# Hybrid decoder layer on one Trainium2 core: the convolution's pointwise weights and its half of the output weights multiplied once on the chip, the second token tile's output projection in one piece, operand transposes issued later

## The chip, the cores and the metric

The kernel runs on one core of a Trainium2 chip. The metric is device time in microseconds (us): the median of three runs before the change is 2017.57 us (2012.16, 2017.57 and 2020.62).

## The reference

One decoder layer over 2048 tokens of width 1024, in float32:

```
hn   = rms_norm(x, mix_pre_g);  proj = hn @ w_in        # 1024 x 1792
attn = sliding-window attention of q, k, v              # 512 columns
u    = the other 1024 columns of proj
conv = silu(layer_norm(depthwise_conv31(a * sigmoid(gate)))) @ w_conv_pw   # 512 x 512
h    = x + rms_norm(concat(attn, conv) @ w_out, mix_post_g)
ff   = (silu(rms_norm(h) @ w_gate) * (rms_norm(h) @ w_up)) @ w_down
out  = h + rms_norm(ff, ffn_post_g)
```

Between the pointwise product with `w_conv_pw` and the product with rows 512 to 1023 of `w_out` there is no other operation.

## The kernel before, in words

**Tiles and precision.** The tokens are four tiles (t = 0 to 3) of 512. Each float32 operand of a large product is held as a high part and a low part (`split_w`, L129: ScalarE copies the high part, GpSimd or VectorE subtracts to get the low part), and a product is three matmuls: high by high, high by low, low by high (`three`, L188). One matmul is 128x128 weights by 128x512. A low part of a weight may be written to memory the first time and read back later (`lo_in`, `lo_out`).

**Stages.** The letter after the @ in a tile's name is the stage, the digit its token tile.
- A0 to A3 (`stage_a`, L327): input projections, 14 units of 24 matmuls each.
- B0 to B3 (`stage_b`, L430): attention in four blocks of 128 tokens. Each block goes through score matmuls, VectorE, exponentials on ScalarE, transposes on TensorE and a mask on GpSimd; its result goes to `mixT[0:4]` in memory.
- C0 to C3: the convolution. `stage_taps` (L563) does 31 taps for each of four channel groups on VectorE and writes to `y_scr`. `stage_tail` and `conv_tail` (L577, L592) load it, transpose on TensorE into the one PSUM bank `ct`, take the statistics, normalise, transpose back, apply swish (`v`, L616), split `v`, and then do the pointwise product: for each of four output groups m, load `w_pw[m]`, split it, 12 matmuls into `ct`, copy out with scale 0.5, write to `mixT[4+m]` from ScalarE's queue (L623 to L631).
- W0 to W3 (`stage_w`, L697): output projection. It walks the eight 128-row blocks of `mixT` and of `w_out` in four pairs `gi` and two column halves n, 24 matmuls each, adding into `acc`; `norm_w` (L747) then norms, adds x and writes `hn_scr`.
- H, F, G (for token tiles 0 and 1, then again, as H2, F2, G2, for 2 and 3): the feed-forward layer, its products arranged in sums of blocks. `stage_h_plain` (L829) makes operands B11 and B21 from `hn_scr` with transposes, `stage_h_sums` (L842, "S0") the others. `stage_pre` (L887) and `stage_p1` are F, `stage_p2` is G.

**What sets the order.** A main line of stages is passed to `run`, and at each of its yields, which carry a nominal time, side lanes (`Lane`, L1275) are pumped: `lb` attention, `lc` taps, `ld` tails C0 and C1, `lw` W0 and later C2, W2, C3, W3, `lh` the H stages and W1's norm (N1), which is offered when W1's last matmul is issued; S0 also waits until F0 has reached its unit 22. A lane works through its items in order and only when an item's condition holds. The order that results is a priority; a scheduler then places the instructions on each engine, and each engine runs its own in that order. The main line is A0 to A3, then W1, then F0 (`stage_pre`, `stage_p1`), G0 and the second half. C0 and W0 run beside A2 and A3, C1 beside A3 and W1, C2, W2, C3 and W3 beside G0.

**W1's stop.** In W1, after the attention half of the rows (`G * gi + G == 4`), the main line runs the first eight units of F0 (`ready`, Q0 = 8, L734 to L740), 12 matmuls each, and in their middle calls `ld.until("C1")`, which issues what is left of C1. Only then does W1 take the convolution half. The rest of F0 follows W1. Because these eight units need operand B11, B11 and B21 are offered to lane `lh` before W1 with no condition (L1417).

Of the kernel before, what the change touches and what calls it, by code (L numbers as in the profile page):

```python
# [23 lines left out]
D = 1024  # L24
DFF = 2816
P = 128
# [11 lines left out]
def layer_kernel(ctx, tc, x, xT, cols, rows, sinks, relb, onehot, w_in, w_pw, w_out, w_gate, w_up, w_down, out):  # L38
# [190 lines left out]

    mixT = dr.tile([KC, P, S], F32, name="mixT")  # L230
    h_scr = dr.tile([S, D], F32, name="h_scr")

    neg = cst.tile([P, 1], F32, name="neg")
    nc.vector.memset(neg, NEG)
# [357 lines left out]
    def conv_tail(t, yt):  # L592
        L = f"C{t}"
        lab[0] = L
        mv = sm(8).rearrange("p (s a) -> p s a", a=2)
        for s in range(4):
            st = sm(6)
            nc.vector.bn_stats(st, yt[:, s])
            nc.vector.bn_aggr(mv[:, s], st)
        r = rsqrt(mv[:, :, 1], 4, 1.0)  # L600
        nmr = sm(4)
        stt(nmr, mv[:, :, 0], -1.0, r, ALU.mult, ALU.mult)
        yield YL if t < 2 else YL2
# [3 lines left out]
        sc = []  # L607
        for c in range(4):
            b = ct()
            for s in range(4):  # L610
                nc.tensor.transpose(b[:, s * P : (s + 1) * P], yt[:, s, c * P : (c + 1) * P], ident)
            th = f2("fc")
            act(th, b, AF.Tanh, scale=lnh[:, c : c + 1], bias=lnh[:, 4 + c : 5 + c])
            v = f2("fc")
            act(v, b, AF.Identity, scale=ln_g[:, c : c + 1], bias=ln_b[:, c : c + 1])
            stt(v, th, 1.0, v, ALU.add, ALU.mult)  # L616
            h = hl("chl")
            act(h[:, 0], v, AF.Copy)
            ptt(h[:, 1], v, h[:, 0].bitcast(F32), ALU.subtract)
            sc.append(h)  # L620
            yield 2
            lab[0] = L
        for m in range(4):  # L623
            raw = f2("fc")
            nc.sync.dma_start(raw, w_pw[m])
            w = split_w(raw, "mb" if t == 1 and m % 2 else "chl").rearrange("p a (k c) -> p a k c", c=P)
            o = ct()
            three(o, [((w[:, 0, k], w[:, 1, k]), (sc[k][:, 0], sc[k][:, 1])) for k in range(4)])
            z = f2("gb" if t > 1 else "fc")
            act(z, o, AF.Copy, scale=0.5)  # L630
            nc.scalar.dma_start(mixT[4 + m, :, t * T : (t + 1) * T], z)  # L631
            yield 2
            lab[0] = L

    bias = []

# [60 lines left out]
    def stage_w(w, spill, G, atag, htag, mtag, bank_of, norm=None, ready=None):  # L697
        L = f"W{w}"
        lab[0] = L
        acc = [f4(atag) for _ in range(4)]  # L700
# [22 lines left out]
        for gi in range(KC // G):  # L723
            aa = nxt
            for n in range(2):
                lab[0] = L
                if n == 0 and w != 1 and gi + 1 < KC // G:
                    rows_next = load(gi + 1)
                if n == 1 and gi + 1 < KC // G and not (ready and G * gi + G == 4):
                    nxt = acts(gi + 1, rows_next if w != 1 else None)  # L730
                ws = weight(w_out[2 * gi : 2 * gi + 2, :, n * T : (n + 1) * T].rearrange("c p t -> p c t"),
                            lo_out[n, 2 * gi : 2 * gi + 2], w > 0)
                yield from block_half(acc, list(zip(aa, ws)), n, gi == 0, L, bank_of)
            if ready and G * gi + G == 4:  # L734
                for i, c in enumerate(ready()):
                    if i == Q0 // 2:
                        ld.until("C1")
                        lab[0] = L
                        nxt = acts(gi + 1)
                    yield c  # L740
        tail = norm_w(w, spill, acc, mtag)
        if norm:
            norm(tail)
# [590 lines left out]
    NS = 12  # L1334
    AHEAD = 3
    PRES = {0: 20, 2: 16}
    Q0 = 8
    POOL_LO = (3, 6)
    PRE_S0, PRE_S2 = 22, 16
    H1, H2, H3, H4 = 0, 4, 7, 11  # L1340
    lb = Lane(RB, 0)
    lc = Lane(RC0, LC)
    lw = Lane(RW0, 0)
# [161 lines left out]
```

## Time and profile before

| what | value |
|---|---|
| median of three runs | 2017.57 us |
| profiled execution, span | 2016.4 us, the only time of it that the profile gives |
| matmuls and transposes in the profiled span | 8826 |
| 128x512 matmuls of the pointwise product (`ct@C`) | 192, 48 for each token tile |
| mean granted TensorE clock | 0.991 of full |
| memory traffic | 223 GB/s over the span |

The span runs from the first to the last instruction. PE is TensorE, PEld its weight loads, DVE is VectorE, ACT is ScalarE, POOL is GpSimd, SP is the engine that issues most transfers. A timeline row gives start, duration, engine, line, operation, tiles out<-in with shape and count, and in brackets the idle time before it with what ended it. A row of windows gives each engine's busy time in a stretch, with the number of instructions, the granted clock and the share of the transfer engines.

### The profile page before, as it was taken

The page shows a single profiled execution, that of the slowest core. Times are in us where ns is not written, and L with a number is a line of the kernel's source. Part 1 is how long each engine was busy: PE and PEld are TensorE (multiplying, and loading weights), DVE is VectorE, ACT ScalarE, POOL GpSimd, SP SyncE. Part 2 cuts the span into 40 slices and gives each one's busy share as a digit, 9 for nine tenths or more (in the row PEclk, how much of TensorE's full clock was granted, in tenths as well). Part 3 has the DMA queues.
Part 4 walks back from the last instruction along what each step waited for, and adds up shares of the span by engine and source line. Part 5 has one row for each costly group of instructions (what it writes and reads, how often), then busy time and mean ns, then how long its engine had stood idle before and what let it go on. Part 6 is the DMA issues. An engine that isn't in the chain of part 4 may idle for free. (4 is left out here: it accounts for less than half of the span.)

```text
span 2016.4 us, 27154 instructions
## 1 busy us (share of the span) xinstructions
PE 1957.8 (97%) x8826; PEld 1563.3 (78%) x8826; DVE 1489.5 (74%) x2679; ACT 985.7 (49%) x1938; POOL 355.0 (18%) x415
## 2 busy tenths in 40 slices
PE   8999999999998999999989999999899999999998
PEld 7877767677667778888878878778688888888886
DVE  5998987985794899888569984475766765545558
ACT  5455455457546633333355466456643343345543
POOL 6000223322110300000001022103523332221000
PEclk9999999999999999999989999999999999999999
DMA  8786645669559878777476778579944443366654
GB/s 309 267 298 221 207 148 175 194 228 322 180 178 325 281 238 269 253 253 254 149 239 216 238 261 283 173 262 348 333 159 167 157 160 107 107 238 214 200 187 162
DMA packets 234110, 451.44 MB, mean 224 GB/s; under 512 B 23496, under 2 KB 49264, under 8 KB 233968
## 3 DMA queue, kind: packets, MB, share of 16 engines
q1 hardware_dynamic: 211184, 411.96, 60.9%
q10 hardware_dynamic: 20544, 30.42, 4.1%
q0 software_dynamic: 2240, 7.34, 0.9%
q8 instruction: 69, 1.13, 0.2%
q14 instruction: 73, 0.60, 0.1%
HBM read 330.60 MB, written 119.02 MB: 223 GB/s over the span
## 5 line engine op out<-in xcount | busy, mean ns | idle before, releaser
L85 DVE SCALAR_TENSOR_TENSOR fc@C<-glu@C,colt,fc@C 128x512 f32<-128x512 f32 x480 | 367.8, 780 | 3.0
L108 PE MATMUL mm@F<-hl@H,w@F 128*128 128x512 f32 x1056 | 254.9, 392 | 5.3 <-ACT mm@F L924 4.9
L108 PEld LDWEIGHTS mm@F<-hl@H,w@F 128*128 128x128 f32 x1056 | 198.5, 189 | 48.8 <-ACT mm@F L924 6.7
L108 PE MATMUL mm@G<-hl@G,hl@G 128*128 128x512 f32 x924 | 228.0, 396 | 6.4 <-DVE x@G L85 4.3
L108 PE MATMUL mm@A<-hl@A,w@A 128*128 128x512 f32 x840 | 206.3, 396 | 3.0 <-ACT hl@A L318 1.2
L108 PEld LDWEIGHTS mm@G<-hl@G,hl@G 128*128 128x128 f32 x924 | 174.1, 190 | 44.5 <-issue 4.1
L797 ACT ACTIVATE w@F<-chl@F 128x512 fp32r<-128x512 f32 x220 | 135.6, 625 | 135.3 <-PE mm@F L108 123.3
L108 PE MATMUL mm@G<-w@G,hl@G 128*128 128x512 f32 x876 | 199.5, 389 | 0.0
L108 PEld LDWEIGHTS mm@G<-w@G,hl@G 128*128 128x128 f32 x876 | 164.4, 188 | 34.1
L108 PEld LDWEIGHTS mm@A<-hl@A,w@A 128*128 128x128 f32 x840 | 154.7, 188 | 39.4 <-DVE hl@A L85 3.0
L85 DVE TENSOR_TENSOR w@F<-chl@F,w@F 128x512 fp32r<-128x512 f32 x198 | 144.9, 733 | 34.7 <-ACT w@F L797 34.3
L108 PE MATMUL mm@F<-mid@H,w@F 128*128 128x512 f32 x528 | 131.1, 393 | 7.4 <-ACT mm@F L924 7.2
L108 PE MATMUL mm@F<-p@H,w@F 128*128 128x512 f32 x528 | 129.1, 389 | 0.8 <-ACT at@F L1046 0.8
L108 PE MATMUL mm@F<-ql@H,w@F 128*128 128x512 f32 x528 | 127.2, 389 | 0.7 <-ACT w@F L797 0.7
L108 PE MATMUL mm@F<-x@H,w@F 128*128 128x512 f32 x528 | 125.5, 391 | 0.0
L108 PEld LDWEIGHTS mm@F<-mid@H,w@F 128*128 128x128 f32 x528 | 98.3, 188 | 30.2 <-ACT mm@F L924 9.0
L108 PEld LDWEIGHTS mm@F<-p@H,w@F 128*128 128x128 f32 x528 | 98.9, 188 | 21.9 <-ACT at@F L1046 1.4
L108 PEld LDWEIGHTS mm@F<-ql@H,w@F 128*128 128x128 f32 x528 | 99.0, 188 | 21.6 <-ACT w@F L797 1.1
L108 PEld LDWEIGHTS mm@F<-x@H,w@F 128*128 128x128 f32 x528 | 98.7, 188 | 21.0
L108 PE MATMUL tr@W<-w@W,ql@W 128*128 128x512 f32 x384 | 103.0, 408 | 8.4 <-ACT ql@W L706 5.1
L133 ACT ACTIVATE w@A<-raw@A 128x512 fp32r<-128x512 f32 x110 | 67.7, 626 | 78.8 <-PE mm@A L108 51.5
L108 PE MATMUL mm@W<-w@W,hl@W 128*128 128x512 f32 x384 | 101.5, 404 | 2.2 <-ACT x@W L679 0.7
(302 smaller groups left out, 3337.0 us busy)
## 6 DMA issues: line engine op xcount, KB each, us to landing
mids<-fa@F SPq DMA_DIRECT2D x154, 256.0 KB, 2.7
raw@A<-w_in SPq DMA_DIRECT2D x55, 512.0 KB, 4.4
w@A<-lo_in SPq DMA_DIRECT2D x84, 256.0 KB, 3.5
fc@G<-mids SPq DMA_DIRECT2D x77, 256.0 KB, 3.5
fa@G<-mids SPq DMA_DIRECT2D x75, 256.0 KB, 4.5
gb@F<-keeps SPq DMA_DIRECT2D x72, 256.0 KB, 4.3
raw@W<-w_out SPq DMA_DIRECT2D x32, 512.0 KB, 5.5
w@W<-lo_out SPq DMA_DIRECT2D x48, 256.0 KB, 4.4
```

The source lines that it names most:

```text
L85: r = op(*args, **kw)
L108: r = nc.tensor.matmul(*args, **kw)
L133: act(w[:, 0], raw, AF.Copy)
L797: act(w[:, 0], x, AF.Copy)
```

## The change

W = 0.5 x `w_conv_pw` @ `w_out[512:1024]` is computed once on the chip, in a new stage J0 of 96 matmuls, and written in eight 128x512 pieces to `w_join` in memory. W0 to W3 read `w_join` where they read rows 512 to 1023 of `w_out`, and the convolution tails write `v` itself to `mixT`; the pointwise product goes. J0 stands in lane `ld` ahead of C0 and starts once A2 has. W1 has no stop, F0 starts at its first unit after W1, and B11 and B21 wait until W0 has been done for a nominal 24 us. On the host `w_conv_pw` is laid out transposed.

```diff
@@ conv_tail
             stt(v, th, 1.0, v, ALU.add, ALU.mult)
-            h = hl("chl")
-            act(h[:, 0], v, AF.Copy)
-            ptt(h[:, 1], v, h[:, 0].bitcast(F32), ALU.subtract)
-            sc.append(h)
+            nc.sync.dma_start(mixT[4 + c, :, t * T : (t + 1) * T], v)
             yield 2
-        for m in range(4):
-            raw = f2("fc")
-            nc.sync.dma_start(raw, w_pw[m])
-            w = split_w(raw, "mb" if t == 1 and m % 2 else "chl").rearrange("p a (k c) -> p a k c", c=P)
-            o = ct()
-            three(o, [((w[:, 0, k], w[:, 1, k]), (sc[k][:, 0], sc[k][:, 1])) for k in range(4)])
-            z = f2("gb" if t > 1 else "fc")
-            act(z, o, AF.Copy, scale=0.5)
-            nc.scalar.dma_start(mixT[4 + m, :, t * T : (t + 1) * T], z)
-            yield 2
+    def stage_join():
+        right = []
+        for k in range(4):
+            raw = f4("wx", (P, 2, T))
+            nc.sync.dma_start(raw, w_out[4 + k].rearrange("p (a b) -> p a b", a=2))
+            yield 1.5
+            for n in range(2):
+                right.append(split_w(raw[:, n], "mid" if k < 2 else "chl"))
+            yield 1.5
+        for mp in range(2):
+            pair_ = t_("yt", (P, 2, 2, T), F32R)
+            raw = f4("wx", (P, 2, T))
+            nc.sync.dma_start(raw, w_pw[2 * mp : 2 * mp + 2].rearrange("m p t -> p m t"))
+            yield 1.5
+            left = [split_w(raw[:, m], pair_[:, m]).rearrange("p a (k c) -> p a k c", c=P) for m in range(2)]
+            yield 2
+            for m in range(2):
+                for n in range(2):
+                    o = ct()
+                    three(o, [((left[m][:, 0, k], left[m][:, 1, k]), (right[2 * k + n][:, 0], right[2 * k + n][:, 1])) for k in range(4)])
+                    z = f2("fa")
+                    act(z, o, AF.Copy, scale=0.5)
+                    nc.scalar.dma_start(w_join[2 * mp + m, :, n * T : (n + 1) * T], z)
+                    yield 4
@@ stage_w
-                if n == 1 and gi + 1 < KC // G and not (ready and G * gi + G == 4):
+                if n == 1 and gi + 1 < KC // G:
+                    if w == 1 and G * gi + G == 4:
+                        ld.until("C1")
                     nxt = acts(gi + 1, rows_next if w != 1 else None)
-                ws = weight(w_out[2 * gi : 2 * gi + 2, :, n * T : (n + 1) * T].rearrange("c p t -> p c t"),
+                src = w_out[2 * gi : 2 * gi + 2] if gi < 2 else w_join[2 * gi - 4 : 2 * gi - 2]
+                ws = weight(src[:, :, n * T : (n + 1) * T].rearrange("c p t -> p c t"),
-            if ready and G * gi + G == 4:
-                for i, c in enumerate(ready()):
-                    if i == Q0 // 2:
-                        ld.until("C1")
-                        nxt = acts(gi + 1)
-                    yield c
@@ the main line
+    ld.add("J", stage_join(), lambda: "A2" in started)
-        lh.add(n + ".0", stage_h_plain(ws, ops, n, off))
-    run(stage_w(1, True, 2, "mid", "hl", "at", mm, norm=lambda g: lh.add("N1", g), ready=lambda: stage_pre(ws, ops, mids[0], keeps[0], 0, Q0)))
+        lh.add(n + ".0", stage_h_plain(ws, ops, n, off), lambda: since(lw, "W0", NH))
+    run(stage_w(1, True, 2, "mid", "hl", "at", mm, norm=lambda g: lh.add("N1", g)))
-    lh.until("B21.0")
-    run(stage_pre(ws, ops, mids[0], keeps[0], Q0))
+    run(stage_pre(ws, ops, mids[0], keeps[0]))
@@ kernel
-    wp = kblocks(f(w_conv_pw))
+    wp = kblocks(f(w_conv_pw).T)
```

More of the change, by code (lines that the diff above doesn't have):

```diff
@@ L231, in layer_kernel @@
     h_scr = dr.tile([S, D], F32, name="h_scr")
+    w_join = dr.tile([4, P, D], F32, name="w_join")
     neg = cst.tile([P, 1], F32, name="neg")
@@ L606, in conv_tail @@
             act(yt[:, s], yt[:, s], AF.Identity, scale=r[:, s : s + 1], bias=nmr[:, s : s + 1])
-        sc = []
         for c in range(4):
@@ L616, in conv_tail @@
             stt(v, th, 1.0, v, ALU.add, ALU.mult)
-            h = hl("chl")
-            act(h[:, 0], v, AF.Copy)
-            ptt(h[:, 1], v, h[:, 0].bitcast(F32), ALU.subtract)
-            sc.append(h)
+            nc.sync.dma_start(mixT[4 + c, :, t * T : (t + 1) * T], v)
             yield 2
             lab[0] = L
-        for m in range(4):
-            raw = f2("fc")
-            nc.sync.dma_start(raw, w_pw[m])
-            w = split_w(raw, "mb" if t == 1 and m % 2 else "chl").rearrange("p a (k c) -> p a k c", c=P)
-            o = ct()
-            three(o, [((w[:, 0, k], w[:, 1, k]), (sc[k][:, 0], sc[k][:, 1])) for k in range(4)])
-            z = f2("gb" if t > 1 else "fc")
-            act(z, o, AF.Copy, scale=0.5)
-            nc.scalar.dma_start(mixT[4 + m, :, t * T : (t + 1) * T], z)
-            yield 2
-            lab[0] = L
+    def stage_join():
+        lab[0] = "J0"
+        right = []
[4 more added lines that the diff above has]
+            for n in range(2):
+                lab[0] = "J0"
+                right.append(split_w(raw[:, n], "mid" if k < 2 else "chl"))
+            yield 1.5
+            lab[0] = "J0"
+        for mp in range(2):
[3 more added lines that the diff above has]
+            yield 1.5
+            lab[0] = "J0"
+            left = [split_w(raw[:, m], pair_[:, m]).rearrange("p a (k c) -> p a k c", c=P) for m in range(2)]
+            yield 2
+            for m in range(2):
+                for n in range(2):
+                    lab[0] = "J0"
+                    o = ct()
[4 more added lines that the diff above has]
+                    yield 4
+                    lab[0] = "J0"
     bias = []
@@ L695, in post_scale, with stage_w @@
             tied(stt(acc[:, cs], acc[:, cs], r, gb[n], ALU.mult, ALU.mult))
-    def stage_w(w, spill, G, atag, htag, mtag, bank_of, norm=None, ready=None):
+    def stage_w(w, spill, G, atag, htag, mtag, bank_of, norm=None):
         L = f"W{w}"
@@ L1336, in layer_kernel @@
     PRES = {0: 20, 2: 16}
-    Q0 = 8
     POOL_LO = (3, 6)
@@ L1340, in layer_kernel @@
     H1, H2, H3, H4 = 0, 4, 7, 11
+    NH = 24
     lb = Lane(RB, 0)
```

2 lines of the change are left out of this document (1 added, 1 removed).

## The prediction

> **What bounds the kernel now.** I read the page first: engine totals, the slices, the chain that ended last.
>
> ```profile
> span 2016.4 us, 27154 instructions
> PE 1957.8 (97%) x8826; PEld 1563.3 (78%) x8826; DVE 1489.5 (74%) x2679; ACT 985.7 (49%) x1938; POOL 355.0 (18%) x415
> PE   8999999999998999999989999999899999999998
> DVE  5998987985794899888569984475766765545558
> PEclk9999999999999999999989999999999999999999
> ```
>
> TensorE is busy 97% of the span and in nearly every slice; no other engine is above 74%. So a matmul more or less costs its own time, and what remains to be won elsewhere is the 58.6 us (2016.4 less 1957.8) in which TensorE sits idle, plus what a lowered clock loses. The next view is the windows of 100 us; columns are the stretch, its length, then busy time and count for each engine, granted clock, transfer share, GB/s.
>
> ```profile
> 200.00:300.00 100.00, 97.12 (x483) 71.48 (x482) 89.38 (x200) 49.58 (x120) 21.20 (x24) 0.98 0.57 184
> 300.00:400.00 100.00, 98.91 (x469) 70.89 (x467) 88.27 (x190) 50.33 (x136) 34.68 (x36) 1.00 0.55 177
> 500.00:600.00 100.00, 92.13 (x435) 67.66 (x436) 85.00 (x179) 51.51 (x126) 10.24 (x12) 0.98 0.55 184
> 1100.00:1200.00 100.00, 97.54 (x432) 79.18 (x431) 95.09 (x154) 46.56 (x85) 9.29 (x17) 1.00 0.75 250
> 1500.00:1600.00 100.00, 100.00 (x443) 82.81 (x442) 65.75 (x85) 39.44 (x70) 31.40 (x21) 1.00 0.47 166
> ```
>
> The row at 1500 has no idle time: 443 matmuls in 100 us, 0.2257 us each. That is my price of a 128x512 matmul that is taken out of or put into a full stretch. The row at 500 (W1 with its stop, C1, B3, the first operand transposes) is the least full of the five. In the row at 1100, beside C2 and the last taps, VectorE is at 95%.
>
> **The change, part by part.** The pointwise matmuls, from the view of their tile, and the splits they need:
>
> ```profile
> L108 PE MATMUL ct@C<-chl@C,chl@C x168: 388/389/795, 288.1 to 1274.0; 128*128 128x512 f32 x168
> L108 PE MATMUL ct@C<-chl@C,mb@C x24: 387/392/502, 499.2 to 525.3; 128*128 128x512 f32 x24
> L135 POOL TENSOR_TENSOR chl@C<-fc@C,chl@C 128x512 fp32r<-128x512 f32 x14 | 19.5, 1396 | 73.6 <-ACT chl@C L133 73.6
> fc@C<-w_pw SPq DMA_DIRECT2D x16, 256.0 KB, 4.6
> ```
>
> 1. *Removed:* 168 + 24 = 192 matmuls, 48 for each token tile. *Added:* J0 has 8 groups of 12, 96. C0's and C1's 96 go from the stretch between 288 and 526 us, and J0's 96 come into A2, in the same stretch or a little ahead of it, where TensorE is 97% to 99% busy: an exchange, 0. C2's and C3's 96 go from G0 without replacement: 96 x 0.2257 = **-21.7 us**. ScalarE, GpSimd and the transfers lose work (28 activations and 20 GpSimd splits fewer, 16 loads of 256 KB replaced by six of 512 KB); they are not the bound, so nothing for that. VectorE's work stays the same.
>
> 2. *What the stops cost now.* TensorE's timeline, in the places that the change touches, and one row after each gap:
>
> ```profile
> 506.96 0.66 PE L815 MATMUL tr@H<-ident,fa@H 128*128 128x128 f32 x4 [2.52 <-ACT gb@H L835]
> 509.46 3.56 PE L108 MATMUL ct@C<-chl@C,chl@C 128*128 128x512 f32 x10 [0.30 <-POOL chl@C L135]
> 523.13 2.54 PE L108 MATMUL ct@C<-chl@C,mb@C 128*128 128x512 f32 x10
> 577.91 0.66 PE L500 MATMUL tr@B<-ident,p@B 128*128 128x128 f32 x4 [3.36 <-DVE p@B L85]
> 581.42 3.01 PE L108 MATMUL mm@W<-w@W,hl@W 128*128 128x512 f32 x12 [0.58 <-DVE hl@W L85]
> 637.31 7.36 PE L108 MATMUL mm@F<-hl@H,w@F 128*128 128x512 f32 x24 [2.75 <-ACT mm@F L924]
> ...
> 1027.69 7.25 PE L108 MATMUL tr@W<-w@W,ql@W 128*128 128x512 f32 x18 [3.27 <-ACT mid@W L679]
> ...
> 1289.51 0.94 PE L108 MATMUL tr@W<-w@W,ql@W 128*128 128x512 f32 x2 [2.15 <-ACT ql@W L706]
> 1290.24 1.49 PE L108 MATMUL mm@G<-hl@G,hl@G 128*128 128x512 f32 x3
> 1291.53 3.98 PE L108 MATMUL tr@W<-w@W,ql@W 128*128 128x512 f32 x13
> 1295.34 3.34 PE L108 MATMUL mm@G<-hl@G,hl@G 128*128 128x512 f32 x14
> ```
>
> A gap costs more than itself, since the clock is lower after it. The ten matmuls at 509.46 took 3.56 us where ten at 523.13 took 2.54: the gap of 2.52 cost 3.5. The 24 at 637.31 took 7.36 against 24 x 0.2257 = 5.4: the gap of 2.75 cost 4.7. The 18 at 1027.69 took 7.25 against 4.1: the gap of 3.27 cost 6.4. From 1289.51 to 1295.34, 18 matmuls took 5.8 against 4.1: the gap of 2.15 cost 3.9. After 3.36 us at 577.91 there is no such loss.
>
> [...]
>
>    - *Operand transposes later, C1's pointwise product gone.* The gap of 2.52 waited for ScalarE's copy of an H0 transpose, queued beside exponentials and C1's copies. In the changed order the same 32 transposes stand in groups of four between runs of W1's matmuls, and W0's `hn_scr` is old by then. I count the gap, its slow clock and some 1.4 us of smaller gaps beside it: **-5**.
>    - *N1 has eight units more.* W1's norm now starts at F0's unit 0 instead of unit 8, so it is out of ScalarE's queue when the second half of the units begins (unit 20), which is where the 2.75 us stood. S0 still begins at unit 22. Between 0 and 4.7 I take half: **-2.3**.
>    - *One hop fewer ahead of W3.* The gap of 2.15 is the end of this chain:
>
> ```profile
> 1278.00 1.00 ACT mm@G L1210 x2
> 1279.00 0.53 ACT gb@C L630
> 1279.55 5.01 DMA mixT<-gb@C
> 1284.62 4.18 DMA at@W<-mixT
> ```
>
>    The write and the read of `mixT` stay (`v` now takes them), but four load-split-multiply-copy rounds through the one bank `ct` go: **-3.9**. Late next is the read of `mixT`, up to 4 us, with G0's own matmuls beside it.
>
> 3. *W1 without its stop.* The eight F0 units, 8 x 12 x 0.2257 = 21.7 us of work that waited for nothing of B3, stood between W1's halves. They are not lost, only later, and B3 now reaches about seven units into F0, so they still cover its last block. But W1's 192 matmuls run beside three blocks of B3 and taps, and B3's chain is what waited at 577.91 while VectorE was full:
>
> ```profile
> 560.00:580.00 20.00, 16.64 (x86) 12.24 (x85) 19.89 (x42) 9.78 (x29) 2.21 (x3) 1.00 0.53 172
> ```
>
>    Ends: 0, if the cover does as well as before, and 21.7, if all of it is lost. Nearest row: one gap more like 577.91, and small ones like 581.42: **+5**.
>
> 4. *J0's waits.* Its 12 weight splits go to ScalarE and GpSimd; at 1.396 us each the latter has 16.8 us more in A2, with 65% or more of its time free. The first `wx` load stands far ahead in SP's queue. What can make TensorE wait: the second pair of `w_pw` groups shares its only buffer (`yt`) with the first, so its splits start when the fourth group is done, and some 26 matmuls (5.9 us) lie between. Ends: 0, and a gap at each of the eight groups, 8 x 6.4 = 51. One short gap is the likeliest: **+2**. C0 behind it: its last transposes stand where W0 has done 48 of its 192 matmuls, and its rows are wanted at 96.
>
> 5. *`mixT` writes on SP.* Two rows carry this one, G0's loads with their time to landing and an issue on SP:
>
> ```profile
> fa@G<-mids SPq DMA_DIRECT2D x75, 256.0 KB, 4.5
> ```
>
> ```profile
> L574 SPq DMA_DIRECT2D y_scr<-fc@C x16: 319/323/633, 116.4 to 1171.9; - x16
> ```
>
>    Sixteen issues of about 0.33 us move from ScalarE's queue to SP's, where each waits for VectorE's `v` with the next weight loads behind it. G0's loads are issued three steps (36 matmuls, 8.1 us) ahead and land in 4.5 or less, so 3.6 us of lateness is hidden. Ends: 0, and one gap of 3.5 for each tile, 14. I take 0.
>
> Sum: -21.7 - 5 - 2.3 - 3.9 + 5 + 2 = **-25.9 us**. The profiled span of 2016.4 becomes 1990.5; it stands 1.2 us under the median shown, so the median becomes 2017.57 - 25.9, about **1992**.
>
> **Rivals.**
> - *The gain in G0 is caught by VectorE, and W1 loses its cover.* C2's 48 matmuls (10.8 us) go from the stretch at 1100 where VectorE is at 95.09 of 100; the same taps in less time would make it the bound. For: that row. Against: in the changed order T3's taps reach some five G0 steps further, and the row at 1500, with VectorE at 66%, shows TensorE full. Price: 8 of the 10.8, and W1 at +12 in place of +5: 1992 + 15 = 2007; 2000 to 2010.
> - *Idle time goes more than I count.* The gap at 1027.69 goes too (6.4), and neither J0 nor W1 brings a new one (7): 1992 - 13 = 1979.
> - *Slower: J0's groups stop TensorE.* TensorE takes its instructions in order, so a split of J0 that is late holds A2 as well. For: one `wx` buffer, one `ct` bank, GpSimd at 1.396 us a split. Against: every group but two uses splits that are old. Price: 51 at eight gaps of 6.4, so 1990 + 51 = 2041. It decides above 2027.7 us, that is from 38 us or six of the eight gaps.
> - *It doesn't save matmul time.* The 96 in G0 lay in time that was lost anyway to the W2 and W3 chains. Against, the stretch of G0:
>
> ```profile
> 1000.00:1340.00 340.00, 324.35 (x1416) 263.90 (x1416) 246.97 (x402) 179.50 (x317) 43.76 (x67) 0.97 0.72 239
> ```
>
>   TensorE is 95% busy there. Then -21.7 becomes about -7, and the new waits take that back: 2012.
>
> **How the numbers follow.** Forecast (1984 to 2000) 0.55; VectorE and W1 0.20; more idle gone 0.13; J0 0.06; no saving 0.06. The range leaves out J0's case and half of the no-saving one, and of the unknown terms takes W1's 21.7 (2017.57 - 21.7 - 5 - 2.3 - 3.9 + 21.7 + 2 = 2008) as its upper end; the lower end is the third case less 2: **1977 to 2008**. A measurement of this kernel tells about 0.5% from no change, 10 us: below 2007.5 is faster. Faster 0.55 + 0.13 + 0.16 of the 0.20 = 0.84; same 0.04 + 0.06 = 0.10; slower 0.06.
>
> **What would show it.** 8730 matmuls and transposes; G0 (first to last matmul before the second half) shorter by about 22 us with its rate unchanged; no gap on an H0 transpose near W1; no gap behind `mixT<-gb@C`; gaps of 2 to 4 us in W1 on B3's tiles; at most one gap on `ct@J`. I am wrong if G0 shortens by less than 15 us, if A2 lengthens by more than J0's 21.7 us and a few, or if W1 and the first units of F0 together show more than 12 us idle.

## The result and the profile after

The changed kernel takes 1998.12 us in the median of four runs (1996.80 to 2003.85), beside 2019.09 us (2012.16 to 2023.10) for the kernel before on the same chip. The ratio is **0.9907, with a 95% interval of 0.9885 to 0.9929**: 0.9% faster, where the forecast said 1992 us. The profiled span went from 2016.4 to 1994.7 us, by 21.7; the forecast of the same difference was 25.9.

The page of the changed kernel, and its windows in the five stretches that the prediction shows for before (start and end, length, busy time and count of each engine, granted clock, transfer share, GB/s):

```profile
span 1994.7 us, 26920 instructions
PE 1939.1 (97%) x8730; PEld 1544.5 (77%) x8730; DVE 1490.7 (75%) x2679; ACT 971.3 (49%) x1910; POOL 332.6 (17%) x395
PE   8999999999899999999999999989999999999998
```

```profile
200.00:300.00 100.00, 95.31 (x460) 68.96 (x457) 95.12 (x206) 41.15 (x109) 23.84 (x17) 0.98 0.56 182
300.00:400.00 100.00, 98.75 (x460) 70.28 (x459) 82.76 (x184) 53.96 (x129) 25.60 (x35) 1.00 0.61 193
500.00:600.00 100.00, 90.75 (x441) 64.94 (x441) 74.30 (x193) 59.22 (x148) 15.40 (x32) 0.95 0.64 213
1100.00:1200.00 100.00, 96.30 (x424) 77.61 (x423) 90.76 (x148) 49.39 (x87) 12.43 (x24) 1.00 0.72 244
1500.00:1600.00 100.00, 100.00 (x443) 82.81 (x442) 66.72 (x86) 40.44 (x72) 34.58 (x23) 1.00 0.48 168
```

The 96 matmuls are gone (8826 to 8730), a full stretch still holds 443 in 100 us, and VectorE at 1100 has not become the bound (95.09 to 90.76). Two stretches got worse: the one at 200, where J0 now runs and VectorE is at 95, and the one at 500, where TensorE's clock is 0.95 in place of 0.98.

Where did the 21.7 us come from? The view of TensorE's tiles gives the first and last start of each group, and with them points that both kernels pass. Three groups of before and the same three of after: F0's unit 20 is the first product on `hl@H`, F0's second part the first on `ql@H`, G0 runs from the first to the last on `hl@G`.

```profile
L108 PE MATMUL mm@F<-hl@H,w@F x1056: 387/389/628, 626.2 to 1786.4; 128*128 128x512 f32 x176
L108 PE MATMUL mm@F<-ql@H,w@F x528: 387/389/501, 693.6 to 1778.3; 128*128 128x512 f32 x176
L108 PE MATMUL mm@G<-hl@G,hl@G x924: 387/389/763, 1006.4 to 1364.6; 128*128 128x512 f32 x185
```

```profile
L108 PE MATMUL mm@F<-hl@H,w@F x1056: 388/389/484, 639.4 to 1764.7; 128*128 128x512 f32 x176
L108 PE MATMUL mm@F<-ql@H,w@F x528: 387/389/794, 697.7 to 1756.5; 128*128 128x512 f32 x176
L108 PE MATMUL mm@G<-hl@G,hl@G x924: 387/389/767, 1014.9 to 1345.0; 128*128 128x512 f32 x185
```

| stretch | before | after | change | forecast |
|---|---|---|---|---|
| start to F0's unit 20 | 626.2 | 639.4 | +13.2 | +2 (-5, +5, +2) |
| unit 20 to F0's second part | 67.4 | 58.3 | -9.1 | -2.3 |
| second part of F0 | 312.8 | 317.2 | +4.4 | 0 |
| G0 | 358.2 | 330.1 | -28.1 | -25.6 (-21.7, -3.9) |
| the rest, to the span's end | 651.8 | 649.7 | -2.1 | 0 |

The sum is near the forecast, the parts are not: the stretch with J0, C1, W1 and the transposes lost 11 us more than forecast, the stretch after it won 7 more. TensorE's timeline of after in these places (start, duration, in brackets the idle time before and what ended it):

```profile
227.04 1.28 PE L108 MATMUL tr@B<-kz,ql@A 64*128 64x256 f32 x12 [3.60 <-DVE sm@B L460]
...
532.85 1.97 PE L108 MATMUL tr@B<-p@B,vtok 128*64 128x512 f32 x4 [3.30 <-ACT p@B L502]
547.04 3.33 PE L108 MATMUL mm@W<-w@W,hl@W 128*128 128x512 f32 x12 [2.52 <-ACT hl@W L723]
...
553.73 3.04 PE L108 MATMUL mm@W<-w@W,hl@W 128*128 128x512 f32 x12 [1.25 <-DVE mid@W L85]
567.49 2.79 PE L108 MATMUL mm@W<-w@W,hl@W 128*128 128x512 f32 x11 [1.09 <-ACT hl@W L723]
...
736.92 1.22 PE L108 MATMUL mm@F<-ql@H,w@F 128*128 128x512 f32 x2 [3.20 <-ACT w@F L811]
...
1027.37 2.93 PE L108 MATMUL tr@W<-w@W,ql@W 128*128 128x512 f32 x6 [3.24 <-ACT ql@W L723]
...
1313.52 6.74 PE L108 MATMUL mm@G<-hl@G,hl@G 128*128 128x512 f32 x21 [6.02 <-DVE x@G L85]
```

The gaps of before at 506.96 (an H0 transpose), 637.31 (three units behind unit 20) and 1289.51 (W3 behind `mixT`) are gone. New are those in W1, and two that the forecast did not have at all: 3.60 us at 227.04, where attention waits for VectorE beside J0, and 3.20 us at 736.92 in F0's second part. The longest of all, 6.02 us at 1313.52 in G0, waits for VectorE and was 3.93 us in before (at 1332.36); no run took it up.

For the comparisons below, a span is split into three: the time that TensorE is idle (span less busy time), the time that the lowered clock takes ((1 - mean granted clock) x span), and the rest, TensorE's work at full clock.

| kernel | span | matmuls | idle | clock | work at full clock |
|---|---|---|---|---|---|
| before | 2016.4 | 8826 | 58.6 | 18 | 1940 |
| changed | 1994.7 | 8730 | 55.6 | 18 | 1921 |

### The profile page after: what moved, and what is told of

It is laid out like the page before. It is cut to its first block, busy times and chain, and to the rows that moved or that the text cites. A ratio compares the mean times of both kernels' runs of the same rounds, so it can differ in the third digit from the quotient of the medians.

```text
span 1994.7 us, 26920 instructions
## 1 busy us (share of the span) xinstructions
PE 1939.1 (97%) x8730; PEld 1544.5 (77%) x8730; DVE 1490.7 (75%) x2679; ACT 971.3 (49%) x1910; POOL 332.6 (17%) x395
## 5 line engine op out<-in xcount | busy, mean ns | idle before, releaser
L108 PEld LDWEIGHTS mm@F<-ql@H,w@F 128*128 128x128 f32 x528 | 99.1, 188 | 25.9 <-ACT w@F L811 5.5
L108 PEld LDWEIGHTS mm@F<-p@H,w@F 128*128 128x128 f32 x528 | 99.9, 190 | 21.7 <-ACT at@F L1060 0.8
L108 PE MATMUL mm@W<-w@W,hl@W 128*128 128x512 f32 x384 | 107.2, 413 | 4.9 <-ACT hl@W L723 3.6
L108 PE MATMUL tr@W<-w@W,ql@W 128*128 128x512 f32 x384 | 98.7, 397 | 4.3 <-ACT ql@W L723 3.4
```

Of the source, the lines that this page charges most:

```text
L108: r = nc.tensor.matmul(*args, **kw)
```

## The experiments

The theory to begin with: the gain is the 96 matmuls and the shorter chain in G0, and the loss ahead of unit 20 is W1 without the eight units of F0 that had covered B3. Ratios are against the kernel before, measured on the same chip (median 2018.39 us for the first four experiments; for the others it stands beside the time).

### The two halves of the change alone, and two variants of it

**The join with the stop** (the changed kernel with before's order):

```diff
-    run(stage_w(1, ..., norm=lambda g: lh.add("N1", g)))
+    run(stage_w(1, ..., norm=lambda g: lh.add("N1", g), ready=lambda: stage_pre(ws, ops, mids[0], keeps[0], 0, Q0)))
-        lh.add(n + ".0", stage_h_plain(ws, ops, n, off), lambda: since(lw, "W0", NH))
+        lh.add(n + ".0", stage_h_plain(ws, ops, n, off))
```

> The join as in the changed kernel, with W1's stop, the eight early units of F0 and the ungated operand transposes of before. Theory 1 (the stretch up to F0's unit 20 grew by 13.2 us because W1 lost the eight units as cover for B3's chain): W1 shows no gap over 2.5 us on a p@B or hl@W tile and unit 20 starts 8 to 11 us earlier than in the changed kernel, at 628 to 631 us; in return the gap of 2.75 us before unit 20 and its followers come back (the stretch after it longer by 5 to 9), so the time is 1990 to 1999, within 4 us of the changed kernel. Rival (J0 in A2 makes the 13.2): unit 20 stays at 637 to 641, the followers come back all the same, and the time is 2003 to 2008.

Measured: 2017.68 us, ratio **0.9992 (0.9975 to 1.0010)**. Both theories missed. Unit 20 starts at 642.1, later than in the changed kernel, so the stop's cover is not what the stretch lost. Where it is lost, the last product of A3 shows, in before and in this kernel:

```profile
L108 PE MATMUL mm@A<-hl@A,w@A x840: 387/389/793, 7.5 to 472.4; 128*128 128x512 f32 x168
```

```profile
L108 PE MATMUL mm@A<-hl@A,w@A x840: 387/389/791, 7.4 to 494.9; 128*128 128x512 f32 x168
```

Up to there the join adds J0's 96 matmuls and takes away C0's 48, which is worth 10.8 us; it costs 22.5. From there to unit 20 it takes away C1's 48, worth 10.8 again; the stretch is 6.6 us shorter. So of the 15.9 us that unit 20 comes later than in before (626.2), 11.7 are lost by the end of A3, where the rival looks, and 4.2 behind it.

96 matmuls fewer in the whole, and no gain. The page's line and the clock:

```profile
PE 1952.6 (97%) x8730; PEld 1553.3 (77%) x8730; DVE 1488.5 (74%) x2679; ACT 970.4 (48%) x1910; POOL 329.8 (16%) x395
```

```profile
core 0: 2018.5 us, clock 0.985
```

The work at full clock is 1922 us, as in the changed kernel. But TensorE is idle for 65.9 us and the clock takes 30: what the matmuls no longer fill has become idle time and slow clock. A part of it, in TensorE's timeline:

```profile
522.07 2.82 PE L833 MATMUL tr@H<-ident,fa@H 128*128 128x128 f32 x12 [2.21 <-ACT gb@H L853]
526.17 0.63 PE L833 MATMUL tr@H<-ident,fa@H 128*128 128x128 f32 x4 [1.28 <-DMA fa@H<-hn_scr]
528.24 1.06 PE L501 MATMUL tr@B<-ident,p@B 128*128 128x128 f32 x4 [1.44 <-ACT gb@H L853]
531.74 1.12 PE L501 MATMUL tr@B<-ident,p@B 128*128 128x128 f32 x4 [2.44 <-ACT gb@H L853]
```

These are the H0 transposes and B3's. Three of the four rows wait for ScalarE's copy of the transposes ahead, the one at 526.17 for the load of `hn_scr`. In before, matmuls of C1's pointwise product stand among the H0 transposes, which end at 513.6 there (the row at 509.46 in the prediction is ten of these matmuls).

**The order alone** (the kernel before, without the stop, transposes since W0 + 24; the reverse of the diff above):

> The kernel before, with only the order changed: no stop in W1, operand transposes once W0 has been done for 24 us; the pointwise product stays as it was. Theory 1: W1 loses its cover here too, so unit 20 of F0 starts 8 to 12 us later than before (634 to 638), the stretch to F0's second part is shorter by 5 to 9, G0 is as before (358 us), and the time is 2014 to 2024, no difference that can be told. Rival (J0 makes the loss, the order only gains): unit 20 at 620 to 628, the stretch after it shorter by 9, time 2003 to 2012.

Measured: 2024.49 us, ratio 1.0034 (1.0020 to 1.0048); unit 20 at 629.8, the stretch after it 69.0 us, not shorter than before's 67.4. Theory 1 and the rival both missed unit 20 and the stretch after it. Slower by itself. So neither half gains, and together they give 0.9%.

**Transposes early** (the changed kernel, with B11's and B21's transposes offered once W0 has begun, near their place in before):

```diff
-    NH = 24
+    NH = 0
```

> The changed kernel with the operand transposes ungated by W0 (offered as soon as W0 has begun), the rest as it is. Theory 1 (B3's chain alone): the gaps in W1 on p@B and hl@W stay, unit 20 within 3 us of 639.4, time 1995 to 2001. Rival (the H0 copies in ScalarE's queue, now beside B3's exponentials in W1, make the gaps): the gaps go from W1, unit 20 starts 5 to 8 us earlier, and the time is 1990 to 1994.

Measured: 2010.52 us, ratio **0.9951 (0.9928 to 0.9974)**. Unit 20 at 650.7, 11.3 us later than in the changed kernel; theory 1 had it within 3 us, the rival 5 to 8 earlier. The H0 transposes are indeed in question, but in the other direction. Its timeline and window:

```profile
521.64 1.09 PE L829 MATMUL tr@H<-ident,fa@H 128*128 128x128 f32 x4 [3.00 <-DMA fa@H<-hn_scr]
...
529.60 3.97 PE L829 MATMUL tr@H<-ident,fa@H 128*128 128x128 f32 x16 [3.64 <-ACT gb@H L849]
```

```profile
520.00:540.00 20.00, 12.25 (x56) 8.51 (x56) 10.91 (x36) 13.24 (x35) 1.59 (x2) 0.63 0.71 230
```

20 us with 12.25 of work at a clock of 0.63. The first gap waits for the load of `hn_scr`, the second for ScalarE's copy. In the kernel before, these transposes run from 495.6 to 513.6, with C1's product beside them, and the 20 us with their gap are

```profile
500.00:520.00 20.00, 16.64 (x78) 12.51 (x78) 11.50 (x26) 15.57 (x39) 4.55 (x5) 0.91 0.70 250
```

**B3 at half its pace**:

```diff
+    lb.rates = {"B3": 0.5}
```

> The changed kernel, with B3's blocks issued at half the pace, so that more of B3 stands beside F0's first units and less in W1. Theory 1: the gaps of 3.30 and 2.52 us in W1 and their slow clock go or shrink, unit 20 starts 5 to 9 us earlier than 639.4, time 1989 to 1994. Rival (the sums of H, which wait for B3's end, come late, and the wait moves to F0's unit 22 and later): W1 gains, but the stretch from unit 20 to F0's second part (58.3 us) is longer by as much or more, time 1997 to 2005.

Measured: 2000.44 us, ratio 0.9908 (0.9882 to 0.9934). The gaps of 3.30 and 2.52 us are gone (the longest between 500 and 640 us is 1.75), the stretch after unit 20 did not suffer (58.2), and yet unit 20 starts at 643.1, 3.7 us later; 2.1 of them are there at A3's last matmul already (498.0 against 495.9). Theory and rival both fail; the last section shows a slow clock that took most of what the gaps gave.

From here the theory was a new one, in two parts. **B**: C1's product was work that TensorE did while the early transposes waited; the join removes it, and only the later transposes close the hole. **C**: in G0 the product's matmuls count only where the rounds of load, split, copy and write around them go too, because the chain C3, W3, N3 bounds G0 as closely as TensorE's work does.

### The price of the matmuls, one place at a time

**C2 and C3 with a third of the product** (the kernel before):

```diff
-            three(o, [((w[:, 0, k], w[:, 1, k]), (sc[k][:, 0], sc[k][:, 1])) for k in range(4)])
+            if t < 2:
+                three(o, ...)
+            else:
+                for k in range(4):
+                    mat(o, w[:, 0, k], sc[k][:, 0], start=k == 0, stop=k == 3)
```

> The kernel before, in which C2's and C3's pointwise product is left with its 32 high by high matmuls (the 64 with a low part are left out, so it computes less than the reference). Theory A (a matmul of the product in G0 stands on the path at its own 0.2257 us): G0 shorter by 64 x 0.2257 = 14.4 us, time 2018 - 14 = 2004, ratio 0.991 to 0.995. Rival (the product in G0 lay in time that gaps and the lowered clock take anyway): G0 shorter by 5 or less, ratio 0.997 to 1.0.

Measured: 2020.30 us beside 2022.51, ratio **0.9979 (0.9958 to 1.0000)**, 4 us of the 14.4. G0 itself is 13.3 us shorter (344.9 from its first to its last matmul), as theory A has it, but the time is the rival's. At F2's first product on B21 only 6 of the 13.3 are left (397.3 us behind G0's start, before 403.3), and the other stretches of the profiled run give back the rest. The four rounds of C3 in TensorE's timeline:

```profile
1254.10 1.07 PE L108 MATMUL ct@C<-chl@C,chl@C 128*128 128x512 f32 x4
...
1260.68 1.07 PE L108 MATMUL ct@C<-chl@C,chl@C 128*128 128x512 f32 x4
...
1267.25 1.07 PE L108 MATMUL ct@C<-chl@C,chl@C 128*128 128x512 f32 x4
...
1274.57 1.09 PE L108 MATMUL ct@C<-chl@C,chl@C 128*128 128x512 f32 x4
```

With 4 matmuls in place of 12 a round takes 6.6 to 7.3 us from its first matmul to the next round's, in before 8.8 to 10.2 (first matmuls at 1243.45, 1253.65, 1262.49 and 1271.56). So the rounds did get shorter, by 7.6 us from the first to the last. But C3's product begins 7.8 us later behind G0's start (244.9 against 237.1), and the last write of the taps ahead of it 12.6 us later (178.1 against 165.5); why, no run says. W3 and N3 follow the last round. N3's writes of `hn_scr`, in before and in this kernel:

```profile
L785 ACTq DMA_DIRECT2D hn_scr<-mid@W x4: 327/327/331, 1362.1 to 1365.9; - x4
```

```profile
L789 ACTq DMA_DIRECT2D hn_scr<-mid@W x4: 326/327/497, 1367.7 to 1370.8; - x4
```

Counted from G0's start (1006.4 and 1009.2) the last one is at 359.5 and 361.6: none of the 14.4 us reached it. In before the end of this chain and TensorE's last matmul of G0 (358.2) are 1.3 us apart, which looks like two bounds at once. What TensorE saved became idle time, 72.0 us in the span against 58.6. In the changed kernel the last write is at 326.0 and the last matmul at 330.1.

**C1 with 4 of its 48 matmuls** (the kernel before):

```diff
+            if t == 1:
+                mat(o, w[:, 0, 0], sc[0][:, 0], start=True, stop=True)
+            else:
                 three(o, ...)
```

> The kernel before, in which C1's pointwise product is left with 4 of its 48 matmuls (the other 44 are left out, so it computes less than the reference); splits, copies and writes stay. Theory B (C1's product was what TensorE did while the early operand transposes waited for ScalarE's copies; without it those waits show): the stretch up to F0's unit 20 gets shorter by 3 us or less in place of 44 x 0.2257 = 9.9, with gaps of 2 us or more on tr@H and tr@B and a lower clock between 505 and 535 us as in the join with the stop; ratio 0.998 to 1.002. Rival (the join with the stop lost its gain by J0 and the order in A2, and C1's product was just work): 8 to 10 us shorter, ratio 0.994 to 0.9965.

Measured: 2019.09 beside 2022.51, ratio 0.9985 (0.9970 to 1.0001). Unit 20 starts at 626.4, before at 626.2. A part of that is chance: A3's last matmul, which stands ahead of the edit, is 2.9 us later in this profile (475.3). From there to unit 20 the stretch is 2.7 us shorter, for 44 matmuls or 9.9 us of work, which is theory B's "3 us or less"; so is the ratio. The gaps are smaller than it said, the longest 1.86 us.

```profile
500.00:520.00 20.00, 13.35 (x63) 9.24 (x63) 12.65 (x32) 16.92 (x42) 5.77 (x5) 0.74 0.79 256
```

13.35 us of work at a clock of 0.74, where before has 16.64 at 0.91: idle time and slow clock together take 11.9 us of these 20, in before 5.2. So 6.7 of the 9.9 us come back as the hole of the two kernels above. Another 3.4 us of slow clock stand ahead of it (last section).

**J0 with a third of its product** (the changed kernel; the same edit in `stage_join`):

> The changed kernel, in which J0's product is left with its 32 high by high matmuls (64 are left out, so it computes less than the reference). If J0's matmuls are paid in full in A2 and A3, as the exchange in the prediction has it: the last matmul of A3 14 us earlier than 493.4, time 1998 - 14 = 1984. Rival (VectorE's taps bound that stretch, and J0's matmuls lie partly in waits for it): 5 to 9 us earlier, time 1989 to 1993.

Measured: 1991.33 us beside 2022.51, ratio 0.9838 (0.9815 to 0.9861). Against the changed kernel's 0.9907 that is 0.7%, 14 us (7 to 21 by the two intervals), and the last matmul of A3 in the tile view is 15.0 us earlier than the changed kernel's 495.9:

```profile
L108 PE MATMUL mm@A<-hl@A,w@A x840: 387/389/793, 7.0 to 480.9; 128*128 128x512 f32 x168
```

The 64 matmuls are paid in full, at 0.22 to 0.23 us each. VectorE at 95 of 100 does not hide them. (The time itself lies in the rival's range, but the kernel before is 3.4 us slower on this chip than in the result.) Yet A3's last matmul is still 8.5 us later than in before, with J0's 32 matmuls against C0's 48: the loss by the end of A3 is not in the number of J0's matmuls.

**The work back in G0, without the rounds** (the changed kernel; nobody reads `o`):

```diff
             nc.sync.dma_start(mixT[4 + c, :, t * T : (t + 1) * T], v)
+            if t > 1:
+                h = hl("chl")
+                act(h[:, 0], v, AF.Copy)
+                o = ct()
+                for k in range(12):
+                    mat(o, h[:, 0, 0:P], h[:, 0], start=k == 0, stop=k == 11)
```

> The changed kernel, in which C2 and C3 again do 96 matmuls of 128x512 (12 for each of the four channel groups, on a rounded copy of the result, read by nobody), without the four rounds of load, split, copy and write. Theory C (in G0 the product's matmuls were paid in full only because W3's chain became shorter at the same time; with the short chain G0 is TensorE's): G0 longer by 96 x 0.2257 = 21.7, time 1998 + 18 to 22 = 2016 to 2020, ratio 0.999 to 1.002. Rival (the short chain alone made the gain in G0, and the matmuls fit into what is idle there): G0 longer by 8 or less, time 2000 to 2006.

Measured: 2020.85 beside 2022.41, ratio **0.9989 (0.9976 to 1.0001)**, 0.8% or 16 us more than the changed kernel; its span is 2019.7, and the work at full clock 1943 us. So the time is theory C's, and the 96 matmuls take the whole gain of the change away again. The places are not theory C's: G0 is 9.6 us longer (339.7 against 330.1), not 21.7, and F2's first product on B21 12.4 (387.7 behind G0's start); 7.1 of the profiled pair's 25 us lie ahead of G0, where the edit puts nothing. Nor did the chain stay short. Each channel group's 12 matmuls take the bank `ct` within C3, and N3's writes are

```profile
L805 ACTq DMA_DIRECT2D hn_scr<-mid@W x4: 326/326/327, 1368.6 to 1371.7; - x4
```

The last is 349.7 us behind G0's start, 326.0 in the changed kernel, 359.5 in before. So this run brings back the matmuls and most of the chain's length together and does not separate them.

**Four empty rounds** (the changed kernel):

```diff
+        for m in range(4 if t > 1 else 0):
+            yield 2
```

> The changed kernel, in which the tails of C2 and C3 again let four rounds of a nominal 2 us pass after their last write, with nothing in them, so that W2 and W3 are issued later by as much as the product's rounds had made them. Theory C (the chain of C3, W3 and N3 sets when the second half's operands come): the first matmul of F2 on B21's operand comes later by 5 to 15 us relative to G0's start (375.3 before the edit), with new idle time ahead of it, time 2002 to 2012. Rival (only the matmuls counted): no later than 3 us, time 1997 to 2002.

Measured: 1999.24 beside 2022.41, ratio 0.9878 (0.9857 to 0.9899), and F2's first product on B21 371.8 us behind G0's start (375.3 in the changed kernel). The later issue costs nothing: of theory C, the part on the order of issue falls. The chain itself did not become longer by it (N3's last write 322.3 us behind G0's start, 326.0 in the changed kernel), so what a longer chain would cost without the matmuls is not tried. That the rounds' load, split, single bank `ct`, copy and write are what held G0 is therefore argued, not shown.

### Two more on what the change brought

**Transposes later still:**

```diff
-    NH = 24
+    NH = 40
```

> The changed kernel with the operand transposes held until W0 has been done for a nominal 40 us in place of 24. Theory B (what counts is that they no longer wait on ScalarE's copies with nothing beside them): unit 20 within 4 us of 639.4, ratio 0.988 to 0.9925, the same as at 24. Rival (the 24 us is a lucky place and each move of them sets new gaps): unit 20 later by 5 us or more, or B21 late for unit 10 and a gap there; ratio 0.993 to 0.997.

Measured: 2009.53 beside 2022.41, ratio 0.9925 (0.9904 to 0.9946), which can't be told from 0.9907; beside the two edits on the same chip that change nothing (the empty rounds, 0.9878, and the GpSimd writes below, 0.9879) it is 0.5% slower. Unit 20 at 640.0, as theory B has it, but the gaps behind it are back: 67.1 us to F0's second part, with

```profile
640.02 3.02 PE L108 MATMUL mm@F<-hl@H,w@F 128*128 128x512 f32 x12 [2.12 <-ACT mm@F L938]
...
669.72 7.17 PE L108 MATMUL mm@F<-hl@H,w@F 128*128 128x512 f32 x24 [2.07 <-ACT mm@F L938]
```

ScalarE's timeline shows what is different. N1's last scaling of rows, in this kernel and in the changed one:

```profile
638.35 1.13 ACT L796 ACTIVATE mid@W<-mid@W,sm@W 128x1024 f32<-128x1024 f32 x1
```

```profile
628.92 1.14 ACT L796 ACTIVATE mid@W<-mid@W,sm@W 128x1024 f32<-128x1024 f32 x1
```

It starts 1.7 us ahead of unit 20 here, 10.5 in the changed kernel, 16.7 with early transposes, 11.3 with a third of J0; with the order alone 5.5 ahead, in before 7.5 behind, in the join with the stop 4.2 behind. In all profiles of this study, the eight kernels with some 10 us or more take 58 to 61 us from unit 20 to the second part, the six with 5.5 or less take 65 to 71. No run moved N1 by itself.

**The gap at 736.92**, in two tries. The weights that TensorE waits for there are split by ScalarE behind a copy of a kept block (an earlier partial sum, read back from memory), and that copy waits for its load:

```profile
735.72 0.60 ACT L1046 ACTIVATE mm@F<-gb@F 128x512 f32<-128x512 f32 x1 [6.91 <-DMA gb@F<-keeps]
```

First, the kept block asked for two products earlier (`fetch(m + 1)` at `nst - 4` in place of `nst - 2`):

> The changed kernel, in which the first part of F's second half asks for the next kept block two products (some 5.4 us) earlier on SP's queue. If the gap of 3.20 us at 736.92 comes from that load standing behind transfers that wait on SP: the gap and its slow clock go (3.2 + 1.7), some of the gaps at 870 and 878 with them, time 1990 to 1995. Rival (the load then meets the same waits, or its buffer is not free): no difference, 1996 to 2000.

Measured: 2002.99 beside 2022.51, ratio 0.9902 (0.9880 to 0.9924); the gap is 3.52 us at 738.90. The load kept its place in SP's queue, behind another that waits, so this edit didn't do what it was meant to. Then the writes that wait taken off SP:

```diff
-                nc.sync.dma_start(td[to, pr], o)
+                nc.gpsimd.dma_start(td[to, pr], o)
```

> The changed kernel, in which the sums of w_down are written to memory from GpSimd's queue and not from SP's; GpSimd has nothing else to do in that stretch. If SP's queue, stopped by these writes until VectorE has the sums, made the kept block late (gap of 3.20 us at 736.92, 1.42 at 878.22 and their slow clock): the gaps go, time 1990 to 1995. Rival (GpSimd's own transfers take longer to issue, or VectorE is slowed by them): 1998 or more.

Measured: 1998.95 beside 2022.41, ratio 0.9879 (0.9857 to 0.9901), which the interval does not tell from the changed kernel; the gap is still there, 4.13 us at 736.95. SP's waits in that stretch (what waited, for what: us, times, longest), first in the changed kernel, then in this one:

```profile
SPq L1107 <- DVE wx@G L85: 3.6, 1, 3.6
```

```profile
SPq L987 <- DVE w@F L85: 6.3, 1, 6.3
```

The write that waited for VectorE is gone from SP's queue, and the next one, a weight load whose buffer VectorE still reads, waits in its place, longer. The kept block stands behind both. No version in this study that does the whole work beats the changed kernel by more than the intervals tell.

## Why the forecast came out

The forecast time was near (1992 against 1998.12, inside the range), the gain of the profiled pair 21.7 against 25.9. That the sum is so near is in part luck: in the five stretches of the table the forecast is off by +11.2, -6.8, +4.4, -2.5 and -2.1 us, which nearly cancel. By its own steps:

1. **C2's and C3's product, -21.7, and one hop fewer ahead of W3, -3.9.** G0 became 28.1 us shorter, so the sum of the two is right. The reason given for the first, "a matmul more or less costs its own time", is not: in the kernel before 64 matmuls were worth 4 us of 14.4, and the 96 put back into the changed kernel cost 16 us with most of the chain's length back as well. The two terms are not independent. The end of the chain of C3, W3 and N3 and TensorE's last matmul of G0 lie close together in both kernels (359.5 and 358.2, 326.0 and 330.1), and the join shortens both. That the chain is what held G0 in before is argued from this; no run shortened the chain and left the matmuls. The rival "it doesn't save matmul time" named the W2 and W3 chains as what could take it; it was set aside because TensorE is 95% busy there, and 95% did not decide it.
2. **C0's and C1's product against J0, 0.** This step failed. With before's order the join puts unit 20 off by 15.9 us (642.1 against 626.2), not 0. Of these, 4.2 lie behind A3: C1's product gave back 6.6 us of 10.8, since it had been what TensorE did while the H0 transposes waited (C1 with 4 matmuls: 2.7 of 9.9). The other 11.7 are lost by the end of A3. J0's matmuls cost 0.22 us each, as priced, and the loss stays when two thirds of them are gone (there mostly as idle time and slow clock). Idle time and slow clock add 3.4 of the 11.7, with the gap of 3.44 us at 224.96 beside J0 (3.60 at 227.04 in the changed kernel; 1.42 at 211.61 in before). The rest is no idle time: TensorE counts as busy for longer. Up to there attention's score matmuls stand in 64 separate groups against 49, and at 0.42 us for each that stands apart (0.73 less 0.31, last section) that is an estimate of 6. What C0's 48 matmuls were worth was not tried, so the cause of the 11.7 stays open. The +13.2 of the table is then 15.9, and 8.6 and -11.3 from steps 5 and 3.
3. **H0's transposes later, -5.** The mechanism is right and the size was not: with the join they are worth 11.3 us at unit 20 and 0.44% of the time (0.9951 against 0.9907, intervals that just overlap). The term was sized by the gap in before, where C1's product covered most of the wait; and a part of the wait is not for ScalarE's copy but for the load of `hn_scr` (3.00 us with the transposes early), which the step took to be old by then. One part of the change took the cover away, another moved what needed it; each was priced against before, and not against the other.
4. **N1's eight units more, -2.3.** The gaps at unit 20 went as a whole: -9.1 us. In before TensorE is idle for 6.0 us of that stretch and its clock is 0.97, in the changed kernel it is not idle there and the clock is 1.00. (The 2.75 us stood three units behind unit 20, not at it: 36 matmuls start between 626.2 and 637.31.) That the missing stop does it is not shown: with the order alone they stay. They go with N1's lead on unit 20, and that depends on the product and the transposes too.
5. **W1 without its stop, +5.** With early transposes the stop can be compared by itself (join with the stop against transposes early): unit 20 comes 8.6 us later without it, the stretch after it is 12.9 shorter, the time 0.41% less. So the stop's end is a gain of some 7 us, with N1's gaps in it, where the steps had +2.7 for both. Gaps of 2 to 4 us in W1 came as forecast, one on B3's tiles (3.30) and one on W1's own `hl@W` (2.52), but slowing B3 removed them without a gain.
6. **J0's waits, +2, and `mixT` writes on SP, 0.** On J0's own tile `ct@J` the changed kernel has no gap over 1 us. That a late operand holds what stands behind it on TensorE, as the rival with J0 had it, shows elsewhere in before: G0's matmuls at 1290.24 read `hl@G`, whose last write before them ended at 1283.23, and started only behind W3's at 1289.51, which waited 2.15 us for `ql@W`. In G0 no gap ends on a transfer of `mixT` or of G0's loads.
7. **F0's second part, 0.** It lost 4.4 us, 3.20 of them in the gap at 736.92, which the steps do not have. Its cause on SP's queue is shown only as far as the two tries go: it is not one write alone.

None of the three signs that were to show the forecast wrong came as they were worded: G0 is shorter by 28.1 us, the last matmul of A3 is later by 23.5, which is J0's 21.7 and 1.8, and W1 with the first units of F0 is idle for 9.1. But the second sign left out that C0's 48 matmuls go from the same stretch. With them, 10.8 us were to be expected there and not 21.7, and 12.7 us of loss lay in sight.

The whole, in ratios: before 1; join with before's order 0.9992; without the stop 0.9951; with the transposes later 0.9907; the order without the join 1.0034. The join removes 96 matmuls in each of the three that have it, and the work at full clock is 1919 to 1922 us in all three (1938 to 1940 in the two without). What differs is idle time and clock: 96, 93 and 74 us. One thing stays open: G0 in the join with the stop is 12.5 us longer up to F2's first product on B21 (387.8 against 375.3) than in the changed kernel, with the same G0 code and longer waits for W3 and C3. It goes with the stop: with early transposes and no stop G0 is 332.7 us from its first to its last matmul, with the stop 343.9. No run says why.

## What to carry to other kernels

A matmul that is removed from a nearly full TensorE can be worth much less than its own time, if a chain beside it ends no earlier (64 in G0, with TensorE 95% busy, were worth 4 us of 14.4) or if something was waiting behind its cover (C1's 44 were worth 2.7 us of 9.9): ask of each removed block what TensorE would have done in that time without it, and take out a part of it alone to see. Parts of one change are not priced one by one against the old profile when one part removes cover and another moves what was covered. A wait at the head of a queue that is removed can show the next one: on SP's queue 3.6 us for `wx@G` went and 6.3 us for `w@F` came.

## What the runs showed of the hardware

**The lowered clock comes without idle time too.** Windows of 4 us in the kernel with the slower B3:

```profile
500.00:504.00 4.00, 4.00 (x13) 2.03 (x12) 3.27 (x8) 2.76 (x5) 2.09 (x7) 0.99 1.04 405
504.00:508.00 4.00, 4.00 (x8) 1.72 (x7) 2.10 (x3) 1.76 (x3) 2.43 (x5) 0.50 0.81 308
508.00:512.00 4.00, 4.00 (x9) 2.68 (x9) 2.69 (x12) 4.00 (x5) 0.00 (x0) 0.50 0.38 154
512.00:516.00 4.00, 4.00 (x14) 3.15 (x13) 0.35 (x1) 2.33 (x5) 0.00 (x0) 0.73 0.86 261
```

TensorE counts as busy throughout, and the clock is halved for 10 us, a loss of 5.1. In the changed kernel the same place (504 to 512) loses 1.7 us, so most of what this kernel's removed gaps gave (idle time between 500 us and unit 20 fell from 9.1 to 5.2) went into it. Just ahead of it, in both kernels, TensorE's order alternates one of attention's score matmuls with one of W1. The rows are the changed kernel's:

```profile
499.08 0.38 PE L108 MATMUL tr@B<-kz,ql@A 64*128 64x256 f32 x1
499.39 0.49 PE L108 MATMUL mm@W<-w@W,hl@W 128*128 128x512 f32 x1
499.81 0.38 PE L108 MATMUL tr@B<-kz,ql@A 64*128 64x256 f32 x1
500.12 0.49 PE L108 MATMUL mm@W<-w@W,hl@W 128*128 128x512 f32 x1
500.55 0.38 PE L108 MATMUL tr@B<-kz,ql@A 64*128 64x256 f32 x1
...
511.58 0.97 PE L108 MATMUL tr@B<-kz,ql@A 64*128 64x256 f32 x12
```

A pair takes 0.73 us from start to start. Twelve score matmuls in a row take 0.97, 0.08 each, and one of W1 0.2257, together 0.31. So more than half of a pair's time is no matmul's own, though the busy column shows none of it as idle. That this lowers the clock is argued from the order of events; no run took the alternation away by itself. The fourteen profiles speak for it: each has such an alternation at the start of W1, without idle time in the 8 us ahead. Where it lasts 5.2 to 5.9 us (before, C2 and C3 with a third of the product, J0 with a third) the clock stays at 1.00; of the eleven where it lasts 6.3 to 10.1, what the slow clock adds included, ten fall to 0.50 and one does not (the GpSimd writes, 7.4). Before has nothing of it, so up to some 5 us of what another profile loses ahead of unit 20 can be this and not its edit. The prediction had looked for the slow clock behind gaps alone. Behind four of the gaps it priced, the granted clock in before is 0.72 (509.4 to 513.4 us), 0.78 (637.3 to 645.0), 0.58 (1027.6 to 1035.0) and 0.82 (1289.5 to 1299.0); behind the 3.36 us at 577.91 it is 1.00 (577.9 to 586.0). What sets the clock is not shown.

**Nearly the same work at a clock between 0.984 and 0.994.** The profiled runs of this study lose 12 to 32 us of a span to the lowered clock, more than most single edits here move. A comparison of two profiles says little before that term is taken out of both.
